# Gates and ups of a decoder block's feed-forward, turned so that the weights move through TensorE

## The chip, the core and the metric

The kernel runs on one core of a Trainium2 chip. It computes one decoder block for 256 tokens of width 2048, in float32 with split products (below), and its metric is the device time of one execution in microseconds. Before the change the median of three runs was 1077.05 us (1076.43 to 1077.9).

## What is computed

The reference is one layer: a normalised input goes through a projection, half of it into a pooling mixer and half into differential attention; both are joined by an output projection, and a gated feed-forward follows. What matters here is the end of it:

```python
mixed = jnp.concatenate([pool_out, attn_out], axis=-1) @ w_out[l]
h = h + rms_norm(mixed, post_mix_norm[l])

hn = rms_norm(h, pre_ffn_norm[l])
ff = (jax.nn.silu(hn @ w_gate[l]) * (hn @ w_up[l])) @ w_down[l]
h = h + rms_norm(ff, post_ffn_norm[l])
```

D_MODEL is 2048, the feed-forward has 5632 columns (44 blocks of 128, or 11 chunks of 512), and there are 256 tokens, worked on as two halves of 128, called t.

## The kernel before, in words

**Products.** Every weight and every activation of a large product is split exactly into a high and a low part of type float32r. A product is then high times high, high times low and low times high, added in PSUM. Weights come in pieces of 512 KB (128 partitions by 1024 columns, `load`, L76) into a ring of six raw buffers; ScalarE (ACT) copies a raw piece to its high part and VectorE (DVE) subtracts that for the low part (`split`, L89 to L92). The parts lie in a ring of three buffers each, named whi and wlo.

**Two forms of product.** In GEMM A (`gemm_a`, L130, and `mm_a`, L123 to L128) the activations are the stationary operand, 128 tokens at a time, and 512 weight columns move: three matmuls of 512 columns for each k (a slice of 128 of the contracted axis) and each half t. The result has tokens in its partitions. In GEMM B (`gemm_b`, L165 to L178) 128 weight columns are stationary and the tokens move; the result has weight columns in its partitions. Its wide form moves the high and the low part of the activations side by side: one matmul of 512 columns (L174, or L177 for the last k) and one of 256 (L175) for each k, in two halves of a PSUM bank, which are added afterwards.

**Order of the stages.** The projections of q, k and v are GEMM A over x; pooling uses the narrow GEMM B; attention works head by head in between. The output projection is GEMM A over mh and ml (`closing`, L543), in four chunks of 512 columns. Of its last chunk, the last 12 k are held in their own tiles (hhi, hlo) and run first over one half of the tokens, then over the other (`gemm_a_skew`, L137), so that h of the first half can be finished and transposed (`h_parts`, L595 to L606) while the other half is computed. The first 512 gate columns are a GEMM A in the same skewed form, with 12 held k, six of them in the ring and six in hhi and hlo.

**Gates and ups.** The other 40 blocks of gates and all 44 blocks of ups are wide GEMM Bs. For each block, ACT copies one half of the bank (L185, L649), DVE adds the other (L186, L650), a row of inverse norms is multiplied in (r3row, made by `as_row`, on DVE in L187 and on POOL in L645), ACT takes SiLU (L644), DVE multiplies gate and up (L657), and the product is split into gh and gl (L660, L661), one tile of each for every block. They have the contracted axis of w_down in their partitions as w_down needs it. Only the first four blocks, whose gates come out of GEMM A, are transposed on TensorE (L654).

**w_down** is `closing` again: GEMM A over gh and gl, four chunks of 44 k, and the final norm.

**What sets the order.** The kernel is written as a plain sequence, and a scheduler orders the instructions of each engine by a simulated timeline; within an engine they run in that order. SyncE's queue (SP) issues nearly all loads, the weights in the order of use.

**Where tiles lie.** Pools are laid out one behind the other: cp (constants, xn, the tiles named gain and sg), ring, acts (x, h), tiny (small things), and then mid (qT, kT, mh, ml), the attention's pool, hold (hhi, hlo) and fp (the feed-forward's own tiles, gh and gl among them), the last ones in turn over the same bytes. In the program of before, ring and acts begin at multiples of 64 bytes, and mid begins at byte 128608, 32 past such a multiple; hold and fp stand likewise.

Of the kernel before, what the change touches and what calls it, by code (L numbers as in the profile page):

```python
# [8 lines left out]
F32 = mybir.dt.float32  # L9
# [17 lines left out]
HOLD = 12  # L27
# behind which held k of w_out's last columns, and of the first gates, which tokens and k of h^T follow
H_OUT = {(1, 6): (0, 0), (1, 8): (0, 1), (1, 10): (0, 2)}
# [3 lines left out]

# 2*pi in parts of 12 bits: a multiple of up to 12 bits of either first part is exact in float32.
TWO_PI = 6.283185307179586
# [8 lines left out]
def block_kernel(ctx: ExitStack, tc: tile.TileContext, x, xT, pos, cols, rows, lamv, invf, invcnt,  # L44
# [24 lines left out]

# [1 line left out]
    latest = [None]  # L71
# [9 lines left out]
    def load_after(dst, src):  # L81
        """A load that is not to be issued before the latest one of weights."""
        with tc.issue_after(latest[0]):
            sync.dma_start(dst, src)
# [18 lines left out]
    def a_steps(srcs, order=None, held=range(0), parts=None):  # L103
        """(index, k, high part, low part) for each k of GEMM A; held: the indices whose parts go as parts(index) says."""
        i = 0
        for s in order or range(len(srcs)):
            raws = [load(srcs[s], half) for half in range(2)]
            for half in range(2):
                by = parts(i) if i in held else ()
                if by != "halves":  # L110
                    hi, lo = split(raws[half], *by)
                for j in range(2):
                    c = slice(j * 512, (j + 1) * 512)
                    if by == "halves":
                        w = split(raws[half][:, c], lambda: (half_tile("wh"), half_tile("wl")))
                    else:
                        w = hi[:, c], lo[:, c]
                    yield i, 4 * s + 2 * half + j, *w
                    i += 1
# [3 lines left out]
    def mm_a(ps, a, t, k, wh, wl, first, last):  # L123
        """[tokens, 512 columns]; a = ah(k, t), al(k, t): the stationary parts."""
        with tc.issue_after(behind[0]) if behind[0] is not None else nullcontext():
            mm.matmul(ps[t][:, :], lhsT=a[0](k, t), rhs=wh, start=first, stop=False)  # L126
            mm.matmul(ps[t][:, :], lhsT=a[1](k, t), rhs=wh, start=False, stop=False)  # L127
            mm.matmul(ps[t][:, :], lhsT=a[0](k, t), rhs=wl, start=False, stop=last)  # L128
# [8 lines left out]
    def gemm_a_skew(srcs, a, nk, order, held_at, parts, hook):  # L137
        """The k of held_at go over the first tokens, then over the others; yields the t that is done.
        hook(t, n): called behind the n-th of them."""
        ps = [bank(), bank()]  # L140
# [23 lines left out]

    def gemm_b(src, x, wide):  # L165
        """[128 columns, tokens], when wide as two addends in the halves of a bank; x(k): the moving parts side by side."""
        ps = bank()
        k = 0
        for hi, lo in pieces(src):
            for j in range(8):  # L170
                c = slice(j * P, (j + 1) * P)
                if wide:
                    if k < NKD - 1:
                        mm.matmul(ps[:, :], lhsT=hi[:, c], rhs=x(k), start=k == 0, stop=False)  # L174
                    mm.matmul(ps[:, 0:S], lhsT=lo[:, c], rhs=x(k)[:, 0:S], start=False, stop=False)  # L175
                    if k == NKD - 1:
                        mm.matmul(ps[:, :], lhsT=hi[:, c], rhs=x(k), start=False, stop=True)  # L177
                else:  # L178
                    mm3(ps[:, 0:S], hi[:, c], lo[:, c], x(k)[:, 0:S], x(k)[:, S:2 * S], k == 0, k == NKD - 1)
                k += 1  # L180
        return ps

    def scaled(dst, ps, row, part):
        """dst <- (sum of the halves) * row"""
        act.activation(part, ps[:, S:2 * S], AF.Copy)  # L185
        dve.tensor_tensor(dst, ps[:, 0:S], part, ALU.add)  # L186
        dve.tensor_tensor(dst, dst, row, ALU.mult)  # L187

# [5 lines left out]
    def rsqrt(v):  # L194
        """1 / sqrt(v), with one Newton step behind the table's square root."""
        n = v.shape[1]
# [12 lines left out]
    def as_row(r, name):  # L209
        """[128, 256] with r's value of each token, the same in all partitions."""  # L210
        ps = bank2()
        for t in range(2):
            rep = small([P, P], tag="rep", bufs=2)
            dve.tensor_copy(rep, r[:, t:t + 1].to_broadcast([P, P]))
            mm.matmul(ps[:, t * P:(t + 1) * P], lhsT=rep, rhs=ident, start=True, stop=True)
        res = cp.tile([P, S], F32, tag=name, name=name)
        dve.tensor_copy(res, ps[:, 0:S])
        return res

# [1 line left out]
    colt = cp.tile([P, 41], F32, name="colt")  # L221
    act.dma_start(colt, cols)
    g1 = lambda k: colt[:, k:k + 1]
    g3 = lambda k: colt[:, 16 + k:17 + k]
    pscale = lambda k: colt[:, 32 + k:33 + k]

    p_mid = ExitStack()
# [46 lines left out]

    # the first chunk of columns, its loads between those of the activations
    ps0 = [bank(), bank()]
# [25 lines left out]

# [1 line left out]
    xsq = ap_.tile([P, S], F32, name="xsq")  # L304
# [69 lines left out]

# [1 line left out]
    def heads_in(ps, scale, what, g):  # L376
# [108 lines left out]
    def pool_u(g):  # L485
# [3 lines left out]
        for ct in range(2):  # L489
            ps = gemm_b(w_u[2 * g + ct], x_k, False)  # L490
            u = ap_.tile([P, 16 + S], F32, tag="u", name=nm("u"), bufs=2)
# [49 lines left out]

# [1 line left out]
    def closing(srcs_of, a, nk, gains, order, tail, parts, hook, done):  # L543
        """h <- h + rms_norm(product) * gain, by chunks c of 512 columns; done(c, t, columns) is called behind each part."""
        sst = small([P, 2, 4], tag="sst", bufs=2)
# [49 lines left out]
    def h_parts(t, c):  # L595
        """The parts of h^T of four k; what mm_a issues from here on stays behind the transposes."""
        tr = bank2() if c % 2 == 0 else psum2.tile([P, 512], F32, tag="hs", name=nm("hs"), bufs=2)
# [21 lines left out]
    def h_hook(at):  # L619
# [3 lines left out]
            h_hook(H_OUT), lambda c, t, z: None)  # L623
    # the first four gates as GEMM A, the first tokens ahead of the others
    a_h = (lambda k, t: hh_k(k)[:, t * P:(t + 1) * P], lambda k, t: hl_k(k)[:, t * P:(t + 1) * P])
    sg = []
    for t, ps in gemm_a_skew([w_g0[i] for i in range(4)], a_h, NKD, None, range(HOLD),
# [3 lines left out]
        act.activation(sg[t], ps[:, :], AF.Silu, scale=rstd3[:, t:t + 1])  # L631
    r3row = as_row(rstd3, "r3row")
    p_hold.close()
    p_mid.close()

# [1 line left out]
    fp = ctx.enter_context(tc.tile_pool(name="fp", bufs=1))  # L637
    gh, gl = [], []
    for j in range(NF):
        if j >= 4:  # L640
            pg = gemm_b(w_gu[2 * j - 4], h_k, True)
            gt = fp.tile([P, S], F32, tag="gt", name=nm("gt"), bufs=2)
            scaled(gt, pg, r3row, fp.tile([P, S], F32, tag="part", name=nm("part"), bufs=2))
            act.activation(gt, gt, AF.Silu)  # L644
            pool.tensor_tensor(gt, gt, r3row, ALU.mult)  # L645
        pu = gemm_b(w_gu[2 * j - 3 if j >= 4 else j], h_k, True)
        gg = fp.tile([P, S], F32, tag="gg", name=nm("gg"), bufs=2)
        part = fp.tile([P, S], F32, tag="part", name=nm("part"), bufs=2)
        act.activation(part, pu[:, S:2 * S], AF.Copy)  # L649
        dve.tensor_tensor(gg, pu[:, 0:S], part, ALU.add)  # L650
        if j < 4:
            tr = bank2()
            for t in range(2):
                mm.transpose(tr[:, t * P:(t + 1) * P], sg[t][:, j * P:(j + 1) * P], ident)  # L654
            gt = fp.tile([P, S], F32, tag="gt", name=nm("gt"), bufs=2)
            dve.tensor_tensor(gt, tr[:, 0:S], r3row, ALU.mult)
        dve.tensor_tensor(gg, gg, gt, ALU.mult)  # L657
        hi = fp.tile([P, S], F32R, name=f"gh{j}")
        lo = fp.tile([P, S], F32R, name=f"gl{j}")
        act.activation(hi, gg, AF.Copy)  # L660
        dve.tensor_tensor(lo, gg, hi.bitcast(F32), ALU.subtract)  # L661
        gh.append(hi)
        gl.append(lo)

    mg_tile = lambda: acts.tile([P, 512], F32, tag="act", name=nm("mg"), bufs=16)
    f_k = (lambda k, t: gh[k][:, t * P:(t + 1) * P], lambda k, t: gl[k][:, t * P:(t + 1) * P])

# [58 lines left out]
```

## Time and profile before

| what | value |
|---|---|
| median of 3 timed runs | 1077.05 us |
| span of the profiled execution, first to last instruction | 1074.6 us |
| TensorE (PE) busy | 1056.4 us, 5477 matmuls |
| DVE busy | 649.2 us |
| ACT busy | 530.2 us |
| POOL busy | 110.7 us |
| read from HBM | 196.27 MB, 185 GB/s over the span |
| mean granted TensorE clock | 0.994 |

The profiled execution isn't one of the timed runs; the profile gives its span and no time of its own, so the table has the two beside each other. In the rows below, "mm<-whi,gh" means an output tile in PSUM and its two inputs, the moving one first, with the tiles' running numbers left out. L126 to L128 are the three matmuls of GEMM A, L174, L175 and L177 those of the wide GEMM B, and L397, L599 and L654 transposes. In a group of instructions the numbers behind the bar are the busy time and the mean time of one in nanoseconds, then the idle time of the engine ahead of them and what ended it.

The matmuls of a GEMM A belong to its stationary tiles: with x to the first projections, with mh and ml to the output projection, with h and hhi or whi to the first gates, with gh and gl to w_down.

### The profile page before, as it was taken

To read this page: it belongs to the slowest core of one execution; us is meant where nothing else is said; L and a number is where in the kernel's file an instruction comes from. 1 tells how busy PE (TensorE), PEld (TensorE's weight loads), DVE (VectorE), ACT (ScalarE), POOL (GpSimd) and SP (SyncE) were. 2 spreads that over 40 slices of the span, in tenths; PEclk is the share of its full clock that TensorE was granted. 3 is DMA by queue.
4 is the path that set the end of the run, shared out by engine and by line. 5 is a ranking of instruction groups with operands and counts; after the bars stand their busy time and mean duration, and the time that the engine had idled before them with its cause. 6 is when DMAs were issued, how large, how long until landed. Compare 5 with 4: busy or idle time off the path is not lost.

```text
span 1074.6 us, 14491 instructions
## 1 busy us (share of the span) xinstructions
PE 1056.4 (98%) x5477; PEld 886.4 (82%) x5477; DVE 649.2 (60%) x881; ACT 530.2 (49%) x782; POOL 110.7 (10%) x113
## 2 busy tenths in 40 slices
PE   7999999999999999999999999999999999999996
PEld 5788888988877888888888888888888888888885
DVE  8847856874666766666566666665665454444554
ACT  5545545654637554545454545454554343343441
POOL 7102300210020010100101101001010000000000
PEclk8999999999999999999999999999999999999998
DMA  7554475456752555555555555555555565556552
GB/s 280 196 178 138 165 265 176 150 173 216 244 180 81 194 187 186 183 190 191 181 186 187 189 184 185 187 192 181 187 196 193 185 199 188 195 190 196 192 177 79
DMA packets 56949, 199.31 MB, mean 185 GB/s; under 512 B 6832, under 2 KB 7728, under 8 KB 56624
## 3 DMA queue, kind: packets, MB, share of 16 engines
q1 hardware_dynamic: 56592, 198.24, 54.8%
q8 instruction: 43, 0.70, 0.3%
q10 hardware_dynamic: 288, 0.15, 0.1%
q14 instruction: 26, 0.21, 0.1%
HBM read 196.27 MB, written 2.10 MB: 185 GB/s over the span
## 4 chain that ended last, share of the span: by engine, by line
PE 95%; DVE 2%; DMA 1%; ACT 0%; SPq 0%; issue 0%; DVEq 0%; ACTq 0%
PE mm L174 27%; PE mm L175 15%; PE mm L128 15%; PE mm L127 15%; PE mm L126 15%; PE mm L177 2%; PE mm L161 2%; PE mm L163 1%; PE mm L162 1%; DVE xn L577 1%; DMA xr<-in_xT 1%; PE sc L420 0%; DVE wlo L298 0%; DMA colt<-in_cols 0%; PE sc L417 0%; PE tr L397 0%
## 5 line engine op out<-in xcount | busy, mean ns | idle before, releaser
L92 DVE TENSOR_TENSOR wlo<-raw,whi 128x1024 fp32r<-128x1024 f32 x343 | 420.5, 1226 | 282.8 <-ACT whi L91 273.1
L91 ACT ACTIVATE whi<-raw 128x1024 fp32r<-128x1024 f32 x343 | 362.8, 1058 | 290.1 <-PE mm L127 197.6
L174 PE MATMUL mm<-h,whi 128*128 128x512 f32 x1260 | 448.9, 399 | 0.0
L175 PE MATMUL mm<-h,wlo 128*128 128x256 f32 x1344 | 364.0, 281 | 0.0
L174 PEld LDWEIGHTS mm<-h,whi 128*128 128x128 f32 x1260 | 236.8, 188 | 54.3
L175 PEld LDWEIGHTS mm<-h,wlo 128*128 128x128 f32 x1344 | 253.7, 189 | 8.4
L126 PE MATMUL mm<-whi,gh 128*128 128x512 f32 x344 | 136.0, 395 | 0.0
L127 PE MATMUL mm<-whi,gl 128*128 128x512 f32 x344 | 135.6, 394 | 0.0
L128 PE MATMUL mm<-wlo,gh 128*128 128x512 f32 x344 | 122.3, 395 | 0.0
L645 POOL TENSOR_TENSOR gt<-gt,r3row 128x256 f32<-128x256 f32 x40 | 52.0, 1300 | 449.0 <-ACT gt L644 449.0
L128 PE MATMUL mm<-wlo,x 128*128 128x512 f32 x192 | 72.6, 402 | 5.2 <-DVE wlo L298 5.2
L126 PEld LDWEIGHTS mm<-whi,gh 128*128 128x128 f32 x344 | 64.5, 188 | 16.0
L128 PEld LDWEIGHTS mm<-wlo,gh 128*128 128x128 f32 x344 | 64.4, 187 | 15.8
L127 PEld LDWEIGHTS mm<-whi,gl 128*128 128x128 f32 x344 | 64.5, 188 | 15.5
L126 PE MATMUL mm<-whi,x 128*128 128x512 f32 x192 | 76.7, 403 | 0.4 <-ACT x L253 0.4
L127 PE MATMUL mm<-whi,x 128*128 128x512 f32 x192 | 76.7, 402 | 0.0
L649 ACT ACTIVATE part<-mm 128x256 f32<-128x256 f32 x44 | 16.9, 384 | 77.5 <-PE mm L177 77.5
L185 ACT ACTIVATE part<-mm 128x256 f32<-128x256 f32 x40 | 15.4, 384 | 73.8 <-PE mm L177 73.8
L128 PEld LDWEIGHTS mm<-wlo,x 128*128 128x128 f32 x192 | 36.8, 194 | 13.9 <-DVE wlo L298 6.0
L126 PEld LDWEIGHTS mm<-whi,x 128*128 128x128 f32 x192 | 37.0, 194 | 9.7 <-ACT x L253 1.4
L127 PEld LDWEIGHTS mm<-whi,x 128*128 128x128 f32 x192 | 37.2, 194 | 8.4 <-DVE x L254 0.7
L650 DVE TENSOR_TENSOR gg<-mm,part 128x256 f32<-128x256 f32 x44 | 18.7, 424 | 39.9 <-ACT part L649 39.9
(203 smaller groups left out, 1069.7 us busy)
## 6 DMA issues: line engine op xcount, KB each, us to landing
raw<-in_w_gu SPq DMA_DIRECT2D x168, 512.0 KB, 3.6
raw<-in_w_down SPq DMA_DIRECT2D x88, 512.0 KB, 4.3
raw<-in_w_in SPq DMA_DIRECT2D x46, 512.0 KB, 3.6
raw<-in_w_out SPq DMA_DIRECT2D x32, 512.0 KB, 3.6
raw<-in_w_u SPq DMA_DIRECT2D x16, 512.0 KB, 3.4
raw<-in_w_g SPq DMA_DIRECT2D x8, 512.0 KB, 5.6
xn<-in_x SPq DMA_DIRECT2D x2, 1024.0 KB, 8.8
gain<-in_rows SPq DMA_DIRECT2D x8, 256.0 KB, 4.3
```

The source lines that it names most:

```text
L91: act.activation(hi, raw, AF.Copy)
L92: (by or dve).tensor_tensor(lo, raw, hi.bitcast(F32), ALU.subtract)
L126: mm.matmul(ps[t][:, :], lhsT=a[0](k, t), rhs=wh, start=first, stop=False)
L127: mm.matmul(ps[t][:, :], lhsT=a[1](k, t), rhs=wh, start=False, stop=False)
L128: mm.matmul(ps[t][:, :], lhsT=a[0](k, t), rhs=wl, start=False, stop=last)
L161: mm.matmul(o, lhsT=wh, rhs=xh, start=st, stop=False)
L174: mm.matmul(ps[:, :], lhsT=hi[:, c], rhs=x(k), start=k == 0, stop=False)
L175: mm.matmul(ps[:, 0:S], lhsT=lo[:, c], rhs=x(k)[:, 0:S], start=False, stop=False)
L177: mm.matmul(ps[:, :], lhsT=hi[:, c], rhs=x(k), start=False, stop=True)
L645: pool.tensor_tensor(gt, gt, r3row, ALU.mult)
L649: act.activation(part, pu[:, S:2 * S], AF.Copy)
L650: dve.tensor_tensor(gg, pu[:, 0:S], part, ALU.add)
```

## The change

All gates and ups become GEMM A, chunk by chunk of 512 columns: the gates of a chunk, then its ups. SiLU, with the token's inverse norm as a scale for each partition, is taken on ACT straight out of PSUM, and one operation of DVE for each half t multiplies the up's bank by the inverse norm and by the gate. The product (gg, tokens in its partitions) is transposed on TensorE in four blocks of 128 for each half, and ACT and DVE split the transposed bank into gh and gl, now one tile of each for a chunk of four blocks. The transposes of a chunk are written behind the next chunk's gates. The wide form of GEMM B, the sums of halves and the row of inverse norms go. The host lays out the weights of gates and ups for GEMM A.

The second edit allocates one small tile more, of 32 bytes, in the pool tiny, and clears it on POOL. The pools behind it then begin 32 bytes further on, and 1024 bytes earlier for the row of norms, which cp no longer holds: mid begins at byte 127616, a multiple of 64, and mh, hhi, gh and all others of these pools stand at multiples of 64 as well. Ring and acts still do.

```diff
-    def gemm_b(src, x, wide):
+    def gemm_b(src, x):
...
-                if wide:
-                    if k < NKD - 1:
-                        mm.matmul(ps[:, :], lhsT=hi[:, c], rhs=x(k), start=k == 0, stop=False)
-                    mm.matmul(ps[:, 0:S], lhsT=lo[:, c], rhs=x(k)[:, 0:S], start=False, stop=False)
-                    if k == NKD - 1:
-                        mm.matmul(ps[:, :], lhsT=hi[:, c], rhs=x(k), start=False, stop=True)
-                else:
-                    mm3(ps[:, 0:S], hi[:, c], lo[:, c], x(k)[:, 0:S], x(k)[:, S:2 * S], k == 0, k == NKD - 1)
+                mm3(ps[:, 0:S], hi[:, c], lo[:, c], x(k)[:, 0:S], x(k)[:, S:2 * S], k == 0, k == NKD - 1)
...
+    pad = small([P, 8], tag="pad", bufs=1)
+    pool.memset(pad, 0.0)
...
-    r3row = as_row(rstd3, "r3row")
...
-    gh, gl = [], []
-    for j in range(NF):
-        if j >= 4:
-            pg = gemm_b(w_gu[2 * j - 4], h_k, True)
-            gt = fp.tile([P, S], F32, tag="gt", name=nm("gt"), bufs=2)
-            scaled(gt, pg, r3row, fp.tile([P, S], F32, tag="part", name=nm("part"), bufs=2))
-            act.activation(gt, gt, AF.Silu)
-            pool.tensor_tensor(gt, gt, r3row, ALU.mult)
-        pu = gemm_b(w_gu[2 * j - 3 if j >= 4 else j], h_k, True)
...
-        act.activation(part, pu[:, S:2 * S], AF.Copy)
-        dve.tensor_tensor(gg, pu[:, 0:S], part, ALU.add)
...
-        dve.tensor_tensor(gg, gg, gt, ALU.mult)
...
-        act.activation(hi, gg, AF.Copy)
-        dve.tensor_tensor(lo, gg, hi.bitcast(F32), ALU.subtract)
...
+    gh = [fp.tile([P, 4, 2, P], F32R, name=f"gh{c}") for c in range(NF // 4)]
+    gl = [fp.tile([P, 4, 2, P], F32R, name=f"gl{c}") for c in range(NF // 4)]
+
+    def g_parts(c, gg):
+        for t in range(2):
+            tr = bank2()
+            for j in range(4):
+                mm.transpose(tr[:, j * P:(j + 1) * P], gg[t][:, j * P:(j + 1) * P], ident)
+            v = tr.rearrange("p (a b) -> p a b", b=P)
+            act.activation(gh[c][:, :, t, :], v, AF.Copy)
+            dve.tensor_tensor(gl[c][:, :, t, :], v, gh[c][:, :, t, :].bitcast(F32), ALU.subtract)
+
+    waiting = None
+    for c in range(NF // 4):
+        if c > 0:
+            ps = gemm_a([w_gu[2 * c - 1, i] for i in range(4)], a_h, NKD)
+            sg = [cp.tile([P, 512], F32, tag="gain", name=nm("sg"), bufs=2) for _ in range(2)]
+            for t in range(2):
+                act.activation(sg[t], ps[t][:, :], AF.Silu, scale=rstd3[:, t:t + 1])
+            g_parts(*waiting)
+        ps = gemm_a([w_gu[2 * c, i] for i in range(4)], a_h, NKD)
+        gg = [fp.tile([P, 512], F32, tag="gg", name=nm("gg"), bufs=3) for _ in range(2)]
+        for t in range(2):
+            dve.scalar_tensor_tensor(gg[t], ps[t][:, :], rstd3[:, t:t + 1], sg[t], ALU.mult, ALU.mult)
+        waiting = c, gg
+    g_parts(*waiting)
...
-    f_k = (lambda k, t: gh[k][:, t * P:(t + 1) * P], lambda k, t: gl[k][:, t * P:(t + 1) * P])
+    f_k = (lambda k, t: gh[k // 4][:, k % 4, t, :], lambda k, t: gl[k // 4][:, k % 4, t, :])
...
-    gate, up = b_pieces(a["w_gate"][0]), b_pieces(a["w_up"][0])
+    gate, up = a_pieces(a["w_gate"][0]), a_pieces(a["w_up"][0])
...
-        "w_gu": cc(np.concatenate([up[:4], np.stack([gate[4:], up[4:]], axis=1).reshape(-1, P, 2048)])),
+        "w_gu": cc(np.stack([gate, up], axis=1).reshape(-1, 4, P, 2048)[1:]),
```

How the scheduler lays this out is seen in the order of the built programs. First TensorE in the middle of the gates and ups, before (names with running numbers: mm a PSUM bank, h the activations of one k, whi and wlo the parts of one weight piece):

```order
L177 MATMUL mm_5638<-h_2347,whi_5663 128x512
L174 MATMUL mm_5692<-h_2332,whi_5697 128x512
L175 MATMUL mm_5692<-h_2332,wlo_5698 128x256
L174 MATMUL mm_5692<-h_2333,whi_5697 128x512
L175 MATMUL mm_5692<-h_2333,wlo_5698 128x256
L174 MATMUL mm_5692<-h_2334,whi_5697 128x512
```

The same stage after the change, at the first transpose of a chunk, 28 matmuls behind the end of its ups (L635 is the transpose in `g_parts`, gg the product, tr a bank for transposes):

```order
L126 MATMUL mm_4444<-whi_4557,h_2346 128x512
L127 MATMUL mm_4444<-whi_4557,h_2346 128x512
L635 MATMUL tr_4593<-ident,gg_4439 128x128
L128 MATMUL mm_4443<-wlo_4558,h_2346 128x512
L128 MATMUL mm_4444<-wlo_4558,h_2346 128x512
L126 MATMUL mm_4443<-whi_4557,h_2347 128x512
```

One bank a block has become two banks a chunk, all matmuls have 512 columns, and a transpose stands alone between two matmuls of a k. Two more such single ones follow after 24 matmuls each, and after 20 more the gates of the next chunk end, where the other five stand together, ahead of that chunk's ups:

```order
L127 MATMUL mm_4444<-whi_4573,h_2349 128x512
L128 MATMUL mm_4444<-wlo_4574,h_2349 128x512
L635 MATMUL tr_4593<-ident,gg_4439 128x128
L635 MATMUL tr_4600<-ident,gg_4440 128x128 x4
L126 MATMUL mm_4607<-whi_4613,h_2334 128x512
L127 MATMUL mm_4607<-whi_4613,h_2334 128x512
```

The transposes of the last chunk stand together behind 20 matmuls of w_down. Second, ScalarE around that same end of a chunk's gates (the banks 4443 and 4444), after the change; before, splits (L91) alternated one by one with a copy or a SiLU of 256 columns:

```order
L91 ACTIVATE whi_4613<-raw_4609 128x1024
L91 ACTIVATE whi_4629<-raw_4611 128x1024
L646 ACTIVATE sg_4589<-mm_4443,rstd_2359 128x512
L91 ACTIVATE whi_4649<-raw_4645 128x1024
L646 ACTIVATE sg_4590<-mm_4444,rstd_2359 128x512
L637 ACTIVATE gh_3332<-tr_4593 128x4x128
L637 ACTIVATE gh_3332<-tr_4600 128x4x128
L91 ACTIVATE whi_4665<-raw_4647 128x1024
```

Two SiLUs (L646) wait for the gates' last matmuls and two copies (L637) for the transposes, and behind them in ScalarE's queue stands the split of the fourth piece of the ups (whi_4665). Third, VectorE at the end of the ups ahead of it (banks 4293 and 4294), after the change:

```order
L92 TENSOR_TENSOR wlo_4450<-raw_4445,whi_4449 128x1024
L92 TENSOR_TENSOR wlo_4466<-raw_4447,whi_4465 128x1024
L651 SCALAR_TENSOR_TENSOR gg_4439<-mm_4293,rstd_2359,sg_4275 128x512
L651 SCALAR_TENSOR_TENSOR gg_4440<-mm_4294,rstd_2359,sg_4276 128x512
L92 TENSOR_TENSOR wlo_4486<-raw_4481,whi_4485 128x1024
```

The products stand behind the splits of the next gates' first two pieces and ahead of the third's. Up to the end of the first gates the order of PE, DVE, ACT and SP is as before, but for what belonged to the row of norms; POOL has the memset ahead of the identity, and no multiplies at the end. SP issues the same number of weight loads of the same size; the load of w_down's first row of gains, whose buffer sg uses too, stands eight weight loads later.

More of the change, by code (lines that the diff above doesn't have):

```diff
@@ L171, in gemm_b @@
                 c = slice(j * P, (j + 1) * P)
-                if wide:
-                    if k < NKD - 1:
-                        mm.matmul(ps[:, :], lhsT=hi[:, c], rhs=x(k), start=k == 0, stop=False)
-                    mm.matmul(ps[:, 0:S], lhsT=lo[:, c], rhs=x(k)[:, 0:S], start=False, stop=False)
-                    if k == NKD - 1:
-                        mm.matmul(ps[:, :], lhsT=hi[:, c], rhs=x(k), start=False, stop=True)
-                else:
-                    mm3(ps[:, 0:S], hi[:, c], lo[:, c], x(k)[:, 0:S], x(k)[:, S:2 * S], k == 0, k == NKD - 1)
+                mm3(ps[:, 0:S], hi[:, c], lo[:, c], x(k)[:, 0:S], x(k)[:, S:2 * S], k == 0, k == NKD - 1)
                 k += 1
         return ps
[L183 to L187, printed above, removed]
     def variance(ss, scale, add=EPS):
@@ L489, in pool_u @@
         for ct in range(2):
-            ps = gemm_b(w_u[2 * g + ct], x_k, False)
+            ps = gemm_b(w_u[2 * g + ct], x_k)
             u = ap_.tile([P, 16 + S], F32, tag="u", name=nm("u"), bufs=2)
@@ L637, in block_kernel @@
     fp = ctx.enter_context(tc.tile_pool(name="fp", bufs=1))
-    gh, gl = [], []
-    for j in range(NF):
-        if j >= 4:
-            pg = gemm_b(w_gu[2 * j - 4], h_k, True)
-            gt = fp.tile([P, S], F32, tag="gt", name=nm("gt"), bufs=2)
-            scaled(gt, pg, r3row, fp.tile([P, S], F32, tag="part", name=nm("part"), bufs=2))
-            act.activation(gt, gt, AF.Silu)
-            pool.tensor_tensor(gt, gt, r3row, ALU.mult)
-        pu = gemm_b(w_gu[2 * j - 3 if j >= 4 else j], h_k, True)
-        gg = fp.tile([P, S], F32, tag="gg", name=nm("gg"), bufs=2)
-        part = fp.tile([P, S], F32, tag="part", name=nm("part"), bufs=2)
-        act.activation(part, pu[:, S:2 * S], AF.Copy)
-        dve.tensor_tensor(gg, pu[:, 0:S], part, ALU.add)
-        if j < 4:
-            tr = bank2()
-            for t in range(2):
-                mm.transpose(tr[:, t * P:(t + 1) * P], sg[t][:, j * P:(j + 1) * P], ident)
-            gt = fp.tile([P, S], F32, tag="gt", name=nm("gt"), bufs=2)
-            dve.tensor_tensor(gt, tr[:, 0:S], r3row, ALU.mult)
-        dve.tensor_tensor(gg, gg, gt, ALU.mult)
-        hi = fp.tile([P, S], F32R, name=f"gh{j}")
-        lo = fp.tile([P, S], F32R, name=f"gl{j}")
-        act.activation(hi, gg, AF.Copy)
-        dve.tensor_tensor(lo, gg, hi.bitcast(F32), ALU.subtract)
-        gh.append(hi)
-        gl.append(lo)
@@ L714 @@
         "w_out": cc(a_pieces(a["w_out"][0])),
-        "w_g0": cc(a_pieces(a["w_gate"][0][:, :512])[0]),
-        "w_gu": cc(np.concatenate([up[:4], np.stack([gate[4:], up[4:]], axis=1).reshape(-1, P, 2048)])),
+        "w_g0": cc(gate[0]),
+        "w_gu": cc(np.stack([gate, up], axis=1).reshape(-1, 4, P, 2048)[1:]),
         "w_down": cc(a_pieces(a["w_down"][0])),
```

## The prediction

> **What bounds the kernel now.** I read the page's first and fourth parts, then TensorE alone in order of time, since what follows turns on a few nanoseconds between matmuls.
>
> ```profile
> PE 1056.4 (98%) x5477; PEld 886.4 (82%) x5477; DVE 649.2 (60%) x881; ACT 530.2 (49%) x782; POOL 110.7 (10%) x113
> PE 95%; DVE 2%; DMA 1%; ACT 0%; SPq 0%; issue 0%; DVEq 0%; ACTq 0%
> ```
>
> TensorE (PE) is busy for 98% of the span and makes up 95% of the chain that ended last. So the time is the number of matmuls times the distance between their starts; the other engines matter only where they would make PE wait. The busy time of a matmul (about 0.40 us here) is no measure of it, since matmuls overlap: the distance of starts is. The chain of waits repeats one row (the last two low-part matmuls) per piece of 512 KB of weights, which is 12 matmuls of 512 columns in a GEMM A:
>
> ```profile
> 130.08 0.45 PE mm L128 x2
> 132.80 0.45 PE mm L128 x2
> ...
> 248.26 0.47 PE mm L128 x2
> 251.06 0.47 PE mm L128 x2
> ...
> 820.62 0.47 PE mm L128 x2
> 823.42 0.47 PE mm L128 x2
> ```
>
> The same code has two paces. In the first projection (rows at 130) a piece takes 2.72 us, 0.2267 us a matmul; in the output projection (248) and in w_down (820) it takes 2.80, 0.2333 a matmul. No engine makes PE wait in any of them. Which tiles meet which pace is seen around the first gates. The timeline has start, length, engine, line and tiles:
>
> ```profile
> 300.33 0.39 PE L126 MATMUL mm<-hhi,mh 128*128 128x512 f32 x1
> ...
> 309.85 0.39 PE L126 MATMUL mm<-hhi,mh 128*128 128x512 f32 x1
> ...
> 334.36 0.40 PE L128 MATMUL mm<-hlo,h 128*128 128x512 f32 x1
> ...
> 336.46 0.40 PE L128 MATMUL mm<-hlo,h 128*128 128x512 f32 x1
> ...
> 340.61 0.39 PE L128 MATMUL mm<-wlo,h 128*128 128x512 f32 x1
> ...
> 343.33 0.39 PE L128 MATMUL mm<-wlo,h 128*128 128x512 f32 x1
> 343.56 0.39 PE L174 MATMUL mm<-h,whi 128*128 128x512 f32 x1
> ...
> 818.82 0.40 PE L174 MATMUL mm<-h,whi 128*128 128x512 f32 x1
> 819.07 0.40 PE L175 MATMUL mm<-h,wlo 128*128 128x256 f32 x2
> 819.30 0.39 PE L177 MATMUL mm<-h,whi 128*128 128x512 f32 x1
> 819.54 0.39 PE L126 MATMUL mm<-whi,gh 128*128 128x512 f32 x1
> ```
>
> In the program of before, the weight ring (whi, wlo) and the tiles of x and h begin at multiples of 64 bytes, while mh, gh and hhi, in the pools behind, begin 32 bytes past one. Moving whi over stationary h, both at 64: 12 matmuls from 340.61 to 343.33, 0.2267 each. Moving hhi over h, one of each kind: 9 from 334.36 to 336.46, 0.2333. Moving hhi over mh, both past: 42 from 300.33 to 309.85, 0.2267. And whi over mh or gh, one of each kind, is the slow 2.80 above. So the pace goes with whether the two operands stand alike, four rows out of four; that is what I build on, though no row here changes an address alone.
>
> **The gates and ups.** The stage runs from the first L174 at 343.56 to the first matmul of w_down at 819.54: 475.98 us for 168 pieces, 2.833 each, with its eight transposes. A piece is eight 512-column and eight 256-column matmuls now and twelve 512-column ones afterwards: equal columns, but fewer instructions, and ring and h both stand at 64 bytes. At 2.72 the 168 pieces take 456.96 us: **-19.02**.
>
> What is added to PE is 88 transposes for 22 blocks of four columns of 128 (the eight of before go with the old stage). Their price, from a run in the first projection and a single one in the present stage:
>
> ```profile
> 70.17 0.39 PE L127 MATMUL mm<-whi,x 128*128 128x512 f32 x1
> 70.40 1.03 PE L397 MATMUL tr<-ident,k 128*128 128x128 f32 x8
> ...
> 73.58 0.39 PE L126 MATMUL mm<-whi,x 128*128 128x512 f32 x1
> ...
> 354.64 0.39 PE L174 MATMUL mm<-h,whi 128*128 128x512 f32 x1
> 354.87 0.27 PE L654 MATMUL tr<-ident,sg 128*128 128x128 f32 x1
> 354.90 0.48 PE L175 MATMUL mm<-h,wlo 128*128 128x256 f32 x2
> 355.22 0.40 PE L177 MATMUL mm<-h,whi 128*128 128x512 f32 x1
> ```
>
> From 70.17 to 73.58 stand 11 matmuls and eight transposes in 3.41 us; the matmuls at 0.2267 are 2.49, which leaves 0.92. In the starts, 0.11 apart, the transposes have 0.109 each (0.87), and 0.046 is lost in the nine matmuls behind them, which run near the slow pace before it settles. A single one costs the same: 354.64 to 355.22 is 0.58, the same matmuls without one (818.82 to 819.30) 0.48. The order of the changed program puts the eight of a chunk in four places: three single ones with 20 to 24 matmuls between, and five together. Ten chunks lie in this stage: 80 times 0.109 and 40 times 0.046, **+10.56**. The last eight stand in w_down.
>
> The Trainium skill, "TensorE: Matmul & The Clock Gate", Part 4 (PE-mode transpose), says that a 128x128 transpose takes about 275 ns in a kernel's context, because TensorE's access to SBUF dominates it. The trace has that figure as a transpose's own length (0.27 in the row of L654) but not as what it holds up the stream; by it, 88 would cost 24.2 us.
>
> **w_down.** 88 pieces at 2.72 instead of 2.80, as gh and gl now start at 64 bytes: -7.04; its eight transposes and one settling: +0.92. Together **-6.12**. They stand behind 20 matmuls of w_down, 4.5 us after the last up, where the product is ready (below).
>
> **Output projection and held gates.** Three chunks of 16 k and four k of the last, six matmuls a k, are 312 with whi over mh, or 26 pieces at 0.08: -2.08. Six held k of the gates (36 with hhi over h) are three pieces more: -0.24. The rest already meet like operands. **-2.32**.
>
> **Covered work.** DVE loses five operations of 256 columns per block and gets four of 512 per chunk; ACT loses its part copies; POOL loses all 40 multiplies (L645) and gets one memset ahead of the identity. I cost these at nothing, since PE hides them:
>
> ```profile
> L92 DVE TENSOR_TENSOR wlo<-raw,whi 128x1024 fp32r<-128x1024 f32 x343 | 420.5, 1226 | 282.8 <-ACT whi L91 273.1 <-PE mm L128 3.1 <-PE tr L474 1.5
> L91 ACT ACTIVATE whi<-raw 128x1024 fp32r<-128x1024 f32 x343 | 362.8, 1058 | 290.1 <-PE mm L127 197.6 <-PE mm L174 73.6 <-issue 8.2
> L379 ACT ACTIVATE k<-mm,r 128x512 f32<-128x512 f32 x4 | 2.7, 682 | 2.1 <-PE mm L128 2.1
> L478 DVE SCALAR_TENSOR_TENSOR ml<-tr,subw,mh 128x512 fp32r<-128x512 f32 x4 | 2.8, 745 | 0.0
> ```
>
> A split is 1.06 us on ACT and 1.23 on DVE in a piece of 2.72, and ACT mostly waits for PE to free a buffer. The new waits: at the end of a gate chunk ACT's queue holds, ahead of the split of the ups' fourth piece, two SiLUs, one split and two copies that wait for the transposes. At 0.68 for a 512-column pass they take 0.68 + 1.06 + 0.68 + 1.36, then the split 1.06: 4.84 us. DVE adds two subtractions (0.75 each) and its split: at most 7.6. PE wants that piece after five transposes and three pieces, 0.55 + 8.16 = 8.7. After a chunk of ups DVE does two products (0.75 each) before the split of the third piece: 2.7 us, wanted after 5.4; the first transpose, 28 matmuls (6.3 us) on, finds them done. The chunk's two PSUM banks are free again a whole chunk before they are wanted. On SP the loads are as many and as large; the first row of gains moves behind eight weight loads, and is used only a chunk later. If this cover failed by 1 us, it would cost 10 us in ten chunks; from the other side, cover can bring no gain, as PE waits for none of it now. What 32 bytes do to the DVE, ACT and POOL work of the attention no row shows; PE is 98% busy, so I take 0 within 1 us either way.
>
> **Sum.** -19.02 + 10.56 - 6.12 - 2.32 = -16.90. The profiled execution's span is 1074.6; the timed runs' median is 1077.05, so some 2.4 us lie around a span. Span after: 1057.7; time **1060.2**. Its own range: without settling 1058; with the slow pace held all along the 77 matmuls around the transposes of a chunk, 10 times 77 times 0.0067, less the 1.84 counted, 1063.5.
>
> **Rivals.**
> *The addresses do nothing*, and w_down and the output projection are slow for another reason. The 9.36 us of the pace there stay away: **1069.5**. For it: addresses never change alone here, and a pace also lags behind a burst. Against: the four combinations.
> *A wait at the chunk's end*: the 1.1 us left on DVE before the fourth piece is wanted isn't enough, say by 1 us each: **1070.2**. Against: ACT and DVE run ahead by three pieces as soon as they can.
> *A transpose holds the stream for its whole 0.27 us*: 88 times 0.16 more, 14.2: **1074.4**. Against: both rows of transposes.
> *The slow pace holds in the gates too* (slower than before). The place is every piece of this stage: 168 at 2.80 is 470.40, 5.58 less than now, and the transposes cost 10.56; w_down stays at its pace and gets 0.92: +5.9, **1083.0**. It decides from 2.765 us a piece, where 475.98 - 10.56 - 0.92 is spread over 168. For it: h with whi is seen settled only from 340 on, and single transposes may keep it unsettled. Against: the first projection's hundreds of matmuls, settled nine behind each burst.
>
> **How the numbers follow.** Forecast 0.70; no address effect 0.10; the wait 0.06; the dear transposes 0.04; slow pace 0.06; others 0.04, half of them at no change. The range goes from 1056.5 (all unknowns at their better end) to 1070.5, which takes in the forecast and the first two rivals, 0.86, with some left for their edges. A measurement of this kernel tells 0.2%, about 2 us, from no change. Faster 0.91, same 0.03, slower 0.06.
>
> **What would show it.** In the profile after: L128 rows of the chain 2.72 apart in the output projection, the gates and w_down, and no idle time of PE with DVE or ACT as its releaser in the new stage, which should last 467.5 us from first gate piece to w_down. 2.80 in w_down means the addresses were not it; 2.80 in the gates turns the sign; transposes that cost more than 0.11 each show as a stage longer than 467.5 with pieces at 2.72.

## The result, and the profile after

The changed kernel takes 1059.89 us, median of four runs (1058.97 to 1061.86), against 1076.74 for the kernel before in the same comparison: a ratio of 0.9847 with a 95% interval of 0.9834 to 0.9861. The forecast was 1060.2. The profiled execution took 1058.97 us, its span is 1057.1. The page after, its first and fourth parts:

```profile
PE 1037.5 (98%) x4881; PEld 858.3 (81%) x4881; DVE 589.7 (56%) x706; ACT 494.8 (47%) x656; POOL 58.1 (5%) x74
PE 95%; DVE 3%; DMA 1%; ACT 0%; SPq 0%; issue 0%; DVEq 0%; ACTq 0%
PE mm L128 29%; PE mm L127 29%; PE mm L126 29%; PE mm L161 2%; PE mm L163 1%; PE mm L162 1%; DVE xn L568 1%; PE tr L635 1%; DMA xr<-in_xT 1%; PE sc L411 0%; DVE wlo L289 0%; PE sc L408 0%; DMA raw<-in_w_in 0%; PE tr L388 0%; DMA colt<-in_cols 0%; PE tr L434 0%
```

TensorE still sets the time, with 596 matmuls fewer, and now nearly all of the chain is the three lines of GEMM A. The chain of waits gives the pace in the output projection (247), in the ups (525) and in w_down (900), start, length and what:

```profile
246.98 0.45 PE mm L128 x2
249.70 0.45 PE mm L128 x2
...
525.57 0.45 PE mm L128 x2
528.29 0.45 PE mm L128 x2
...
900.03 0.45 PE mm L128 x2
902.75 0.45 PE mm L128 x2
```

All three are 2.72 us a piece; the first and the last were 2.80. Whether PE waits in the new stage is read from the windows view (length, then busy time and number of instructions of PE, PEld, DVE, ACT and POOL, clock, DMA):

```profile
340.80:808.20 467.40, 467.40 (x2097) 385.39 (x2096) 234.04 (x217) 204.99 (x216) 0.00 (x0) 1.00 0.57 189
```

PE is busy for every microsecond of it: ACT and DVE are at 0.44 and 0.50 of the stretch, and no idle time of PE is seen. Matmuls overlap here (0.39 us long, 0.227 apart), so a wait shorter than 0.16 us would not show as idle time; but the stage's length leaves no room for many, with 456.96 us for the pieces and 10.56 for the transposes, 467.52 in all, against 467.49. The stage's ends are in the timeline of PE, the first gate chunk's last matmul being the one at 340.56:

```profile
340.56 0.39 PE L128 MATMUL mm<-wlo,h 128*128 128x512 f32 x1
340.79 0.39 PE L126 MATMUL mm<-whi,h 128*128 128x512 f32 x1
...
808.05 0.39 PE L128 MATMUL mm<-wlo,h 128*128 128x512 f32 x1
808.28 0.39 PE L126 MATMUL mm<-whi,gh 128*128 128x512 f32 x1
```

The following table has the stages of the two profiled executions as distances between the starts of their first matmuls, with the term of the prediction beside them.

| stretch | before, us | after, us | difference | predicted |
|---|---|---|---|---|
| to the first matmul of the projections | 5.92 | 5.13 | -0.79 | 0 |
| projections, pooling, attention | 215.16 | 215.18 | +0.02 | 0 |
| output projection up to the held part | 76.50 | 74.72 | -1.78 | -2.08 |
| held part and first gates | 45.99 | 45.76 | -0.22 | -0.24 |
| the other gates, and the ups | 475.98 | 467.49 | -8.49 | -8.46 |
| w_down, first to last matmul | 246.16 | 240.05 | -6.10 | -6.12 |
| from there to the end | 8.93 | 8.82 | -0.11 | 0 |
| span | 1074.62 | 1057.15 | -17.47 | -16.90 |

### The profile page after: what moved, and what is told of

Read it like the earlier page. It is cut to its first block, busy times and chain, and to the rows that moved or that the text cites. A ratio compares the mean times of both kernels' runs of the same rounds, so it can differ in the third digit from the quotient of the medians.

```text
span 1057.1 us, 12801 instructions
## 1 busy us (share of the span) xinstructions
PE 1037.5 (98%) x4881; PEld 858.3 (81%) x4881; DVE 589.7 (56%) x706; ACT 494.8 (47%) x656; POOL 58.1 (5%) x74
## 4 chain that ended last, share of the span: by engine, by line
PE 95%; DVE 3%; DMA 1%; ACT 0%; SPq 0%; issue 0%; DVEq 0%; ACTq 0%
PE mm L128 29%; PE mm L127 29%; PE mm L126 29%; PE mm L161 2%; PE mm L163 1%; PE mm L162 1%; DVE xn L568 1%; PE tr L635 1%; DMA xr<-in_xT 1%; PE sc L411 0%; DVE wlo L289 0%; PE sc L408 0%; DMA raw<-in_w_in 0%; PE tr L388 0%; DMA colt<-in_cols 0%; PE tr L434 0%
## 5 line engine op out<-in xcount | busy, mean ns | idle before, releaser
L91 ACT ACTIVATE whi<-raw 128x1024 fp32r<-128x1024 f32 x343 | 363.1, 1059 | 455.4 <-PE mm L127 437.7
L126 PE MATMUL mm<-whi,h 128*128 128x512 f32 x692 | 270.7, 391 | 0.0
L127 PE MATMUL mm<-whi,h 128*128 128x512 f32 x692 | 269.7, 390 | 0.0
L128 PE MATMUL mm<-wlo,h 128*128 128x512 f32 x692 | 248.5, 394 | 0.0
L126 PEld LDWEIGHTS mm<-whi,h 128*128 128x128 f32 x692 | 129.9, 188 | 27.0
L127 PEld LDWEIGHTS mm<-whi,h 128*128 128x128 f32 x692 | 129.9, 188 | 27.0
L128 PEld LDWEIGHTS mm<-wlo,h 128*128 128x128 f32 x692 | 127.7, 188 | 27.8
L126 PE MATMUL mm<-whi,gh 128*128 128x512 f32 x344 | 133.8, 389 | 0.0
L127 PEld LDWEIGHTS mm<-whi,gl 128*128 128x128 f32 x344 | 64.6, 188 | 13.4
L127 PE MATMUL mm<-whi,ml 128*128 128x512 f32 x104 | 40.5, 390 | 0.0
L126 PE MATMUL mm<-whi,mh 128*128 128x512 f32 x104 | 40.1, 390 | 0.0
```

The costliest lines, as they stand in the source:

```text
L91: act.activation(hi, raw, AF.Copy)
```

## The experiments

Three questions were open. Is it the addresses that set the pace, and is it being alike or being a multiple of 64? What does a transpose cost, and what its place? And does the gain of the gates come from turning the product, or from something else in the old form? All ratios are against the kernel before.

**Without the 32-byte tile** (e1). The turn alone:

```diff
-    pad = small([P, 8], tag="pad", bufs=1)
-    pool.memset(pad, 0.0)
```

> The changed kernel without the 32-byte tile: mh, hhi, gh and gl stand 32 bytes past a multiple of 64 again, ring, x and h at multiples. If the pace goes with whether the two operands stand alike: pieces of w_down 2.80 us apart (+6.8 us against the changed kernel, whose w_down takes 240.05), output projection about 76.3 us instead of 74.5, gates and ups unchanged at 467.5: some 9 us slower than the changed kernel, 1069. If addresses do nothing and the new shape of gh and gl made w_down faster: 1060.

1070.54 us, ratio 0.9938 (0.9923 to 0.9954). The chain shows 2.80 in the output projection and in w_down, and 2.72 in the ups between them:

```profile
247.76 0.47 PE mm L128 x2
250.56 0.47 PE mm L128 x2
...
528.04 0.45 PE mm L128 x2
530.76 0.45 PE mm L128 x2
...
905.50 0.47 PE mm L128 x2
908.30 0.47 PE mm L128 x2
```

w_down takes 247.04 us from first to last matmul, the output projection 76.50, gates and ups 468.1. The new shape of gh and gl does nothing for w_down; the 32 bytes do it all.

**The 32-byte tile alone** (e2), in the kernel before:

```diff
+    pad = small([P, 8], tag="pad", bufs=1)
+    pool.memset(pad, 0.0)
```

> The kernel before with the 32-byte tile alone, gates and ups still wide GEMM Bs. Operands alike: w_down 2.72 a piece, 239.5 us instead of 246.2, output projection 74.5 instead of 76.3, gates and ups unchanged at 476.0 since ring and h stood at 64 already: 9 us faster than before, 1068. If the gain of w_down came from the new layout of gh and gl or from what runs ahead of it: no change, 1077.

1067.04 us, ratio 0.9916 (0.9895 to 0.9938). Gates and ups stay at 475.93 us; the output projection takes 74.56 and w_down 239.14. The chain of w_down, with the feed-forward ahead of it unchanged:

```profile
899.97 0.45 PE mm L128 x2
902.69 0.45 PE mm L128 x2
```

So the two edits nearly add up: of the 16.9 us between the medians, the tile alone brings 9.6 and the turn alone 6.1 (1076.66 less each kernel's median), 15.7 together. The 1.2 us between are less than the spread of e1's four runs (1068.78 to 1071.57); by the spans of the profiled executions it is 9.3 and 7.6, of 17.5.

**All tiles shifted by 32 bytes** (e3), on top of the changed kernel:

```diff
     pool.memset(pad, 0.0)
+    cpad = cp.tile([P, 8], F32, name="cpad")
+    pool.memset(cpad, 0.0)
```

> The changed kernel with 32 bytes more at the start, so that all tiles, weight ring, x, h, mh, gh, hhi and the identity, stand 32 bytes past a multiple of 64. If only being alike counts: every piece 2.72 as in the changed kernel, 1060. If a multiple of 64 itself counts: 2.80 or more a piece everywhere, 330 pieces by 0.08 is +26 us, 1086 or worse.

1060.45 us, ratio 0.9846 (0.9832 to 0.9861), level with the changed kernel. The weight ring, x, h, mh, gh, hhi and the identity stand 32 bytes past a multiple of 64, and every pace is the fast one (the output projection, at 75.71 us, has a wait in it, see below):

```profile
526.79 0.45 PE mm L128 x2
529.51 0.45 PE mm L128 x2
...
901.25 0.45 PE mm L128 x2
903.97 0.45 PE mm L128 x2
```

Multiples of 64 are not what counts. The two operands of a GEMM A must stand alike. How far alike is open: in the built programs the two operands of every fast GEMM A have the same place within 256 bytes, and those of every slow one lie 32 bytes apart in it. No run sets them 64 or 128 apart, so that 64 bytes are the right measure is not shown.

**The weight ring 32 bytes off** (e4), with x, h, mh, hhi and gh left at multiples of 64. It is e3 with one tile more in the ring. Some tiles of cp, the identity among them, are 32 off as in e3; none of them is an operand of a GEMM A:

```diff
     pool.memset(pad, 0.0)
+    cpad = cp.tile([P, 8], F32, name="cpad")
+    pool.memset(cpad, 0.0)
...
+    rpad = ring.tile([P, 8], F32, tag="rpad", name="rpad", bufs=1)
+    pool.memset(rpad, 0.0)
     ones = cp.tile([P, 1], F32, name="ones")
```

> The changed kernel with the weight ring alone 32 bytes past a multiple of 64, x, h, mh, gh and hhi at multiples. Operands unlike in every GEMM A: gates and ups 168 pieces at 2.80 instead of 2.72, +13 us in that stage (481), w_down 246, output projection 76.3, first projections up to +4: about 1086. It is also the slow rival of the prediction made on purpose: slower than the kernel before by some 9 us. If it isn't the moving operand's address against the stationary one's: 1060.

1083.5 us, ratio 1.006 (1.004 to 1.0081): slower than before, with all the work of the change done as written, if less so than the 1086 expected. Now even the gates and ups run at 2.80:

```profile
536.72 0.47 PE mm L128 x2
539.52 0.47 PE mm L128 x2
...
906.56 0.47 PE mm L128 x2
909.36 0.47 PE mm L128 x2
```

Gates and ups take 478.70 us, 11.2 more than in the changed kernel. 168 pieces by 0.08 would be 13.4; most of the rest isn't lost because around the transposes the pace was slow already (1.8 us of settling in the changed kernel). w_down takes 246.93, the output projection 76.62, the stretch from the first projection up to it 219.6 instead of 215.2. That the total is so near the prediction's slow rival (1083.0) is partly chance: against the kernel before, the gates and ups are 2.7 us longer, where the rival had 5.0, and 4.4 us come from the first projections, which it left as they were.

**Transposes in one place** (e5). A chunk's transposes are held behind the next chunk's gates:

```diff
+    newest = [None]
...
-            mm.matmul(ps[t][:, :], lhsT=a[0](k, t), rhs=wl, start=False, stop=last)
+            newest[0] = mm.matmul(ps[t][:, :], lhsT=a[0](k, t), rhs=wl, start=False, stop=last).ins
...
-                mm.transpose(tr[:, j * P:(j + 1) * P], gg[t][:, j * P:(j + 1) * P], ident)
+                with tc.issue_after(newest[0]):
+                    mm.transpose(tr[:, j * P:(j + 1) * P], gg[t][:, j * P:(j + 1) * P], ident)
```

> The changed kernel, with the eight transposes of a chunk held back behind the next chunk's gates, so that they stand in one place and not in four. If a burst of transposes costs 0.109 us each and some 0.045 of settling for each place: 30 places fewer, the stage of gates and ups 466.1 us instead of 467.5, the whole about 1.4 us faster than the changed kernel, 1058.5. If single transposes cost no settling: 467.5 and 1060. If eight in one place make ACT and DVE late (their copies all fall behind the gates): idle time of PE in the profile and a longer stage.

The stage takes 465.89 us instead of 467.49; the whole 1059.21 us, ratio 0.9833 (0.9819 to 0.9846). The gain of 1.6 us is plain in the stage; the timed runs can't tell the kernel from the changed one, and in its profile a wait in the output projection takes 0.8 of it back (see below). The chain around a burst:

```profile
430.45 0.23 PE mm L129
430.68 0.87 PE tr L637 x8
431.55 0.23 PE mm L127
431.79 0.23 PE mm L128
```

Eight transposes hold up the stream for 0.87 us, and PE doesn't wait for the copies behind them.

**Each transpose twice** (e6), into the same place, so that the output stays what it was:

```diff
                 mm.transpose(tr[:, j * P:(j + 1) * P], gg[t][:, j * P:(j + 1) * P], ident)
+                mm.transpose(tr[:, j * P:(j + 1) * P], gg[t][:, j * P:(j + 1) * P], ident)
```

> The changed kernel, with each of the 88 transposes of the products issued twice into the same place, so that the output is the same. At 0.109 us each: the stage of gates and ups 476.2 us instead of 467.5, w_down +0.9, the whole +9.6, about 1069.5. If a transpose holds up the stream for its length of 0.27 us: +24, about 1084.

1070.57 us, ratio 0.9935 (0.9917 to 0.9953). The stage is 476.09 us long: 8.60 more for 80 more transposes, 0.1075 each. The timeline has them 0.11 apart, with a length of 0.27 each:

```profile
432.47 0.27 PE L636 MATMUL tr<-ident,gg 128*128 128x128 f32 x1
432.58 0.27 PE L635 MATMUL tr<-ident,gg 128*128 128x128 f32 x1
432.69 0.27 PE L636 MATMUL tr<-ident,gg 128*128 128x128 f32 x1
```

The length that the Trainium skill gives for a transpose in a kernel, about 275 ns ("TensorE: Matmul & The Clock Gate", Part 4), is a length here too, 0.27 us, and no price.

**The old form, sorted by size** (e8). GEMM B with the 32-byte tile; of each piece the eight matmuls of 512 columns run in a row and the eight of 256 in a row, and no product is turned:

```diff
+            if wide:
+                cs = [slice(j * P, (j + 1) * P) for j in range(8)]
+
+                def narrow():
+                    for j, c in enumerate(cs):
+                        mm.matmul(ps[:, 0:S], lhsT=lo[:, c], rhs=x(k + j)[:, 0:S], start=False, stop=False)
+
+                if k > 0:
+                    narrow()
+                for j, c in enumerate(cs):
+                    mm.matmul(ps[:, :], lhsT=hi[:, c], rhs=x(k + j), start=k + j == 0, stop=k + j == NKD - 1)
+                if k == 0:
+                    narrow()
+                k += 8
+                continue
             for j in range(8):
                 c = slice(j * P, (j + 1) * P)
-                if wide:
...
```

> The kernel before with the 32-byte tile, and gates and ups still as wide GEMM B, but of each weight piece the eight 512-column matmuls in a row and the eight 256-column ones in a row, instead of in turn. If a matmul has 0.0133 us beside its columns and the other 0.053 us of a piece come from two sizes in turn: a piece 2.773 us instead of 2.826, 168 pieces 465.9, the stage about 467 with its transposes: 9 us faster than with the tile alone, 1058, level with the changed kernel. If the 0.11 us a piece were all from sixteen instructions instead of twelve: no gain, 1067.

1060.74 us, ratio 0.9845 (0.9832 to 0.9859), level with the changed kernel. Its stage takes 468.99 us (467 was expected), 7.0 less than before (475.98), with the same matmuls in another order. The timeline of PE in the old order, here with the tile alone (e2), and in the new one (e8):

```profile
599.63 0.40 PE L174 MATMUL mm<-h,whi 128*128 128x512 f32 x1
599.87 0.28 PE L175 MATMUL mm<-h,wlo 128*128 128x256 f32 x1
...
600.69 0.40 PE L174 MATMUL mm<-h,whi 128*128 128x512 f32 x1
```

```profile
406.50 2.08 PE L175 MATMUL mm<-h,wlo 128*128 128x256 f32 x16
408.41 0.86 PE L180 MATMUL mm<-h,whi 128*128 128x512 f32 x3
```

In turn, three pairs take 1.06 us (599.63 to 600.69), 0.353 each. From 406.50 to 408.41 sixteen matmuls of 256 columns take 1.91 us, 0.119 each (0.120 once they have settled); the 512-column ones between them are back at 0.227 after some five. Over the stage a pair took (475.98 / 168) / 8 = 0.354 in turn, and it takes (468.99 / 168) / 8 = 0.349 sorted, transposes in both. The sum of 0.2267 and 0.120 is 0.3467; the 3 us above it (eight times 168 times 0.0023) are the stage's transposes and the settling at 84 changes of size.

The edit also parts the high weights from the low ones, which stood in turn as the sizes did. That isn't what it gains by: in the narrow GEMM B of the kernel before, high and low weights stand in turn at one size, and the starts are 0.120 apart.

```profile
205.74 0.28 PE L163 MATMUL mm<-x,wlo 128*128 128x256 f32 x1
205.86 0.28 PE L161 MATMUL mm<-x,whi 128*128 128x256 f32 x1
...
206.34 0.28 PE L162 MATMUL mm<-x,whi 128*128 128x256 f32 x1
```

## Why the prediction held, point by point

**What bounds the kernel.** TensorE's stream did, and does. The term for each stage that the change touches came out within 0.3 us, and the total was missed by 0.3 us. Part of that is luck. 0.79 us came from a start that was earlier, ahead of any work that the change touches: in the nine profiled executions it lies between 5.13 and 6.01 us, and the changed kernel's is the lowest. The output projection was lucky too (below). The 2.4 us around a span were a median set against the span of another execution; in every run whose span is on record it is 1.7 to 1.9. The forecast doesn't hang on it, being the median before less 16.90.

**The pace and the addresses.** This was an inference from four combinations of tiles, none of which moved an address alone. The runs made it a shown cause, by moving addresses with no other edit: 1070.54 without the 32 bytes, 1067.04 with them alone, 1060.45 with all operands shifted together, 1083.5 with the ring shifted against the others. The rule is the one that the prediction stated, being alike, though within how many bytes is not shown (e3). Which part of the chip needs it these runs do not tell.

**Gates and ups.** 168 pieces at 2.72, and PE idle nowhere: -8.49 for -8.46. The number held, but its cause is only half of what the prediction named. It put the -19.02 down to fewer instructions; it had measured the old stage's 2.833 a piece, in which the cost of two sizes in turn was contained unseen. Sorted, the same matmuls would take 1344 times 0.3467, or 465.9 us, and turned 456.96: about 9 us are the four instructions fewer a piece, and most of the other 10 are the sizes in turn, which go without turning anything. Sorting alone brought 7.0 of the 8.5 us with as many instructions as ever; turning the product does both, but pays 10.56 us for transposes and settling, and is left with 1.5 more.

**Transposes.** 0.1075 us each by doubling them, for 0.109; settling, 30 places fewer are 1.6 us less, or 0.053 a place, for 0.046. That 0.046 was right as a mean alone: in the starts of the changed kernel a single transpose has 0.051 of settling and five together 0.031, and (30 times 0.051 + 10 times 0.031) / 40 is 0.046. The rival with 0.27 each is out.

**Waits.** The chance of a wait at the chunk's end was priced from a margin of 1.1 us on DVE. It did not come: the stage is PE from end to end, and even eight transposes in one place cost none.

**Output projection: mis-sized.** -1.78 for -2.08. The term counted every matmul at the fast pace. Two things were left out. One is settling, behind the three groups of smaller matmuls that interrupt the stage: e2, where TensorE does not wait there, gained 1.94. The other is a wait that was not there before. The held weights of the last chunk are fetched along with those in use, and with PE quicker their loads come late. It costs 0.1 us in the changed kernel's profile and 1.1 us in that of the all-shifted kernel (e3), whose chain shows it:

```profile
286.21 6.69 DMA raw<-in_w_out
292.90 0.03 issue
292.93 0.02 DVEq L92
292.95 0.04 issue
292.99 1.23 DVE wlo L92
294.22 0.04 issue
294.26 0.73 PE mm L128 x2
```

A load of 512 KB lands 6.7 us behind its issue, where the median of this run's loads of the same weights is 4.2, and TensorE waits for the split behind it. The windows view of the same stretch, before and in e3:

```profile
288.00:295.00 7.00, 7.00 (x31) 5.62 (x30) 6.34 (x6) 5.80 (x10) 0.00 (x0) 1.00 0.90 303
```

```profile
288.00:295.00 7.00, 6.43 (x27) 4.70 (x26) 6.00 (x6) 5.32 (x9) 0.00 (x0) 1.00 0.95 356
```

The DMA engines were busy at 0.90 before (the last two numbers are their share and GB/s), and are at 0.95 in e3 and 0.93 in the changed kernel. That the transfers bound these 7 us is a reading, and no run tested it: loads of up to 5.8 us stand here before, and of 7.1 in e2, and TensorE did not wait. The wait came in four of the six profiled kernels with the quick pace in this stage (e3 1.1 us, e5 0.9, e6 1.2, e8 0.9), and was at most 0.2 in the three with the slow one. Those four take 75.45 to 75.74 us here, so that some 1 us of the 1.78 was luck. The transposes of h, some 15 us further on, wait for DVE as they did before.

## What to carry to other kernels

Where TensorE is busy throughout, read the distance between the starts of matmuls, stage by stage, and compare stages that run the same code: a difference of 3% is a cause to be found, and here one of 32 bytes of padding removed it. Let the stationary and the moving operand of a product stand at like addresses (the same place within 256 bytes was enough here, 32 bytes apart was not), keep equal sizes together in the stream, and keep transposes together. Before turning a product for fewer instructions, sort the instructions that are there: it gave the same time here, without the 88 transposes of the turned product.

## What the runs showed of the hardware that was not expected

- A matmul of 512 float32r columns starts 0.2267 us after the one ahead, or 0.2333 when the addresses of its two operands lie 32 bytes apart within 256. Both 32 bytes past a multiple of 64 is as fast as both at one. Other distances were not run.
- 256 columns take 0.119 to 0.120 in a row of their kind. Where both sizes stand in turn, a pair takes 0.353 (2.826 us a piece divided by eight, from the 452.01 us between the first and the last of 2560 matmuls in the timeline of e2) rather than 0.347.
- Behind a single transpose in the changed kernel the pace needs some nine matmuls to settle, 0.05 us in all. Behind five together there, and behind eight together in e5, it needs some three, 0.02 to 0.03 us. A burst of eight in the first projection has 0.04 in the changed kernel and 0.02 in e5, so the length of the burst does not decide it; what does is not shown.
- A stage of 467 us in which TensorE is never idle has room: ACT at 0.44 and DVE at 0.50. TensorE waits elsewhere: in most kernels with the quick pace for a load in the 7 us ahead of the held part of the output projection.
